# Two-layer hybrid encoder: splits of the left factors placed two products apart, two of them in the down stage, the down stage's first weights fetched and split inside the last pair

## The chip, the cores and the metric

The kernel runs on one core of one Trainium2 chip. The metric is device time of one execution in microseconds (us). Five engines work side by side, each through its own instructions in program order: TensorE (PE, matmuls; its weight loads are listed as PEld), VectorE (DVE), ScalarE (ACT), GpSimd (POOL) and SyncE (SP, which here issues DMA transfers). POOL issues DMA transfers too. A matmul writes to PSUM banks; ACT and DVE copy from there to SBUF.

## The reference, cut to what matters

Two layers, each a token mixer (Fourier mixing, spatial gating, attention) and then a SwiGLU channel mixer, on x of 1024 positions by 1024 channels in float32. The change touches the channel mixer alone:

```python
D_MODEL, SEQ, DEPTH, D_FF = 1024, 1024, 2, 2816

def swiglu(h, w_gate, w_up, w_down):
    return (jax.nn.silu(h @ w_gate) * (h @ w_up)) @ w_down

for l in range(DEPTH):
    ...
    h = rmsnorm(x, g_pre_ffn[l])
    f = swiglu(h, w_gate[l], w_up[l], w_down[l])
    x = x + rmsnorm(f, g_post_ffn[l])
```

## The kernel before, in words

Every float32 factor is split into a rounded high part and the low rest (`split`: a cast on ACT, line 127, then a subtraction on DVE, line 128), and each product is three matmul passes (`matmul3`, line 152): high by high, high by low, low by high. Large products are multiplied by a Strassen scheme with seven products instead of eight.

The channel mixer of a layer has two stages. The **ff stage** computes gate and up in 11 pairs p = 0 to 10 of 256 hidden columns. A pair is 14 products n = 14p + j: j // 2 is the Strassen product v (0 to 6), j % 2 chooses gate or up. `ff_prod(n)` issues 12 matmuls of 128x512 into PSUM tiles fx (the running sum X) or fy (Y and Z); `ff_post(n)` brings them to SBUF: for v = 0, 3 and 4 ACT copies X (line 1050) into a place in the large tile `nat`, and PE goes on adding to the same bank only after that copy. `ff_prep(n + 6)` splits the weights `w_f` of a product six ahead (raw weights `raw_f` lie in a pool `rawp` of 4 buffers).

The result of a pair becomes the left side of the **down stage**. `left_sums` (line 992, on POOL at j = 1 and 3 of the following pair) forms sums of its four blocks, and `left_split(p, k)` splits the seven left factors k = 0 to 6 of pair p; we write 9/k3 for factor 3 of pair 9. The high part goes to one of two places HIS in `nat`, in turn, the low part replaces the source, and `store_a` stores both to a DRAM scratch `asp` (line 986, SP queue, 256 KB each). Since there are two HIS places, a split's cast must wait until the stores of the split two before it have landed. Factors of pair 10 go another way: both parts into one `rawp` buffer, tile `ls`, stored with one transfer of 512 KB, and their splits run in the down stage.

The tables LSTEPS say after which product a split is written in the program. In the last pair they stand at other products than in the ones before. The program is reordered afterwards: a planner with costs of its own moves each engine's instructions, as far as data and order edges allow. `run` leaves the planner free, `run_behind` adds an order edge: what it issues stays, on its engine's queue, behind the instructions written last before it on PE, ACT, DVE and POOL. An order edge is no wait on the chip.

The down stage multiplies by w_down in four groups of 2, 3, 3 and 3 pairs and seven Strassen products each (steps s = 0 to 27). `d_load` fetches 512 KB of w_down into tiles `dr` (line 1080, SP queue); `d_left(s)` fetches stored left factors into tiles `da` (line 1090, POOL queue, 512 KB for each pair); `d_prep(s)` forms the sums of `dr` (line 1100, DVE) and splits them into `dw`; `d_prod` multiplies (PSUM tiles fX, fY), and ACT (line 1144) or DVE (line 1146) brings results to `nat`. Step 0 uses pairs 0 and 1, whose factors were stored long before. The `dr` and `da` tiles take the memory of the ff stage's right factors B11, B21, T1 to B22 (tiles hB, hT), one after the other as these are used up. The table DLOADS says at which of the last products they are fetched: the first four `dr` and the first two `da` are written into the last pair.

Of the kernel before, what the change touches and what calls it, by code (L numbers as in the profile page):

```python
# [81 lines left out]
def encoder_kernel(ctx, tc, A, out):  # L82
# [43 lines left out]
    def split(hi, lo, src, eng=nc.vector):  # L126
        nc.scalar.copy(hi, src)  # L127
        eng.tensor_tensor(out=lo, in0=src, in1=hi.bitcast(F32), op=ALU.subtract)  # L128
# [126 lines left out]
    @contextmanager  # L255
    def behind(*engines):

        with ExitStack() as s:
            ins = nc.cur_bb.bb.instructions
            for eng in engines or (nc.tensor, nc.scalar, nc.vector, nc.gpsimd):  # L260
                prev = next((i for i in reversed(ins) if i.engine == eng.engine), None)
                if prev is not None:
                    s.enter_context(tc.issue_after(prev))
            yield

    def run_behind(*steps):
        with behind():
            run(*steps)
# [15 lines left out]
    def run(*steps):  # L284
        for s in steps:
            s[0](*s[1:])
# [77 lines left out]
    for l in range(DEPTH):  # L364
# [446 lines left out]
        for m in range(1, len(groups)):  # L811
            for j in range(4):
                s = max(8 * m + 2 * j - 9, 0)
# [3 lines left out]
        for n, G in enumerate(groups):  # L817
# [4 lines left out]
            for kt in range(NT):  # L822
                s = 8 * n + kt
# [89 lines left out]
        NPAIR = NFF // 2  # L913
        NPROD = 14 * NPAIR
# [22 lines left out]
        def ff_load(p, m, kh):  # L937
            w = A[("w_gate", "w_up")[m]]
            raws[p, m, kh] = fetch(w[l, kh * 512:(kh + 1) * 512, p * 256:(p + 1) * 256].rearrange("(k p) n -> p k n", p=P), [4, 256],
                                   f"f{l}_{p}_{m}_{kh}")  # L940
# [20 lines left out]
        def ff_prep(n):  # L961
            if n >= NPROD:
                return
            if n + 2 < NPROD and n % 14 < 12:
                ff_sums(n + 2)
            p, j = divmod(n, 14)
            v, m = j // 2, j % 2
            a11, a21, a12, a22 = blocks_of(p, m)
            wv[n] = wsplit((a11, a12, sums.get((p, m)), a11, a21, a22, a12)[v], [4, P], f"f{l}_{n}")
# [6 lines left out]
        def place(i, half):  # L976
            return nat[:, i, half * 512:(half + 1) * 512]
# [4 lines left out]
        def store_a(p, v, x, t, n=1):  # L982

            gi = next(g for g in range(len(DGROUPS)) if p in DGROUPS[g])
            dst = asp[asp_rows(gi, v, p - DGROUPS[gi][0], x, n), :]
            nc.sync.dma_start(dst if n == 1 else dst.rearrange("(x p) n -> p x n", p=P), t)
# [17 lines left out]
        def left_split(p, k):  # L1004

            v, key, m = LEFTS[k]
            t = pq["s", p] if m is None else pq[key, p, m]
            if p == NPAIR - 1:
                w = rawp.tile([P, 2, 512], R32, tag="raw", name=f"ls{l}_{p}_{k}")
                split(w[:, 0], w[:, 1], t)  # L1010
                store_a(p, v, 0, w.bitcast(F32), 2)
                return
            hi = place(*HIS[hin[0] % 2]).bitcast(R32)
            hin[0] += 1
            lo = t.bitcast(R32)
            split(hi, lo, t)
            store_a(p, v, 0, hi.bitcast(F32))
            store_a(p, v, 1, t)

        def ff_prod(n):  # L1020
            p, j = divmod(n, 14)
            v, m = j // 2, j % 2
            if v == 0:
                pq["X", p, m] = psx(f"fx{l}_{n}")
            if v in (1, 2):
                pq["YZ"[v - 1], p, m] = ps1(f"fy{l}_{n}")
            ps = pq["X", p, m] if v in (0, 3, 4, 5) else pq["Y" if v == 1 else "Z", p, m]
            new = v in (0, 1, 2)
            b = hv[RHS[v]]
            for k in range(4):  # L1030
                matmul3(ps, lambda x: wv[n][:, x, k, :], lambda y: b[:, y, k, :], new and k == 0, k == 3, skip_group_check=not new)

        def ff_post(n):
            p, j = divmod(n, 14)
            v, m = j // 2, j % 2
            X = pq["X", p, m]

            def finish(key, acc):

                t = pq[key, p, m]  # L1040
                nc.vector.tensor_tensor(out=t, in0=acc, in1=t, op=ALU.add)  # L1041
                if m == 0:
                    nc.scalar.activation(t, t, AF.Silu)
                else:
                    nc.vector.tensor_tensor(out=t, in0=pq[key, p, 0], in1=t, op=ALU.mult)

            if v in (0, 3, 4):
                key = ("p1", None, None, "u2", "u3")[v]
                t = pq[key, p, m] = pc(p, key, m)
                nc.scalar.copy(t, X)  # L1050
            if v == 1:
                finish("p1", pq["Y", p, m])
            elif v == 4:
                finish("u3", pq["Z", p, m])
            elif v == 5:
                if m == 0:
                    t = pq["s", p] = pc(p, "s")
                    nc.scalar.activation(t, X, AF.Silu)
                else:
                    t = pq["s", p]  # L1060
                    nc.vector.tensor_tensor(out=t, in0=X, in1=t, op=ALU.mult)
            elif v == 6:
                finish("u2", pq["Z", p, m])
# [6 lines left out]
        def d_unit(kind, i, shape, dt, name):  # L1070
            p = du[kind]
            return p.tile([P] + shape, dt, tag=f"{kind}{i}", name=name, bufs=1)
# [19 lines left out]
        def d_blk(gi, pi, b):  # L1092

            r, c = divmod(b, 10)
            return draw[gi, pi, r - 1][:, (c - 1) * 512:c * 512]

        def d_sums(gi, v):
            for pi in range(len(DGROUPS[gi])):
                w = lambda b: d_blk(gi, pi, b)
                tt = lambda o, x, y: nc.vector.tensor_tensor(out=o, in0=x, in1=y, op=ALU.subtract)  # L1100
                if v == 5:
                    tt(w(11), w(12), w(11))
                    tt(w(12), w(22), w(12))
                elif v == 6:
                    tt(w(11), w(22), w(11))
                elif v == 4:
                    tt(w(21), w(21), w(11))
# [6 lines left out]
        def d_prep(s):  # L1114
            if s >= len(STEPS):
                return
            gi, v = STEPS[s]
            d_sums(gi, v)
            for pi in range(len(DGROUPS[gi])):
                nm = f"dw{l}_{s}_{pi}"  # L1120
                if gi + 1 < len(DGROUPS) or v not in DSLOT:
                    t = Wp.tile([P, 2, 512], R32, tag="w", name=nm)
                else:
                    kind, i = DSLOT[v]
                    t = d_unit(kind, i + pi, [2, 512], R32, nm)
                split(t[:, 0], t[:, 1], d_blk(gi, pi, DRIGHT[v]))
                dop[s, pi] = t
# [38 lines left out]
        for t in range(2, NT):  # L1166
# [11 lines left out]
            if t == 7:  # L1178
# [3 lines left out]
                q = res[t]  # L1182
# [19 lines left out]
                  6: ((t_split, "T4", 0), (ff_prep, 12)), 7: ((t_split, "T4", 1), (ff_prep, 13)),  # L1202
                  8: ((t_split, "B22", 0),), 9: ((t_split, "B22", 1),)}

        LSTEPS = {(False, j): ((q, k),) for j, q, k in ((4, 1, 0), (6, 1, 1), (8, 1, 2), (10, 1, 3), (12, 1, 4), (0, 2, 5), (2, 2, 6))}
        LSTEPS.update({(True, j): ((q, k),) for j, q, k in ((4, 1, 0), (5, 1, 1), (7, 1, 2), (8, 1, 3), (9, 1, 4), (11, 1, 5), (12, 1, 6), (0, 2, 5), (2, 2, 6))})
        DLOADS = {0: ((d_load, 0, 0), (d_load, 0, 1)), 1: ((d_left, 0),), 2: ((d_load, 0, 2),), 3: ((d_load, 0, 3),), 5: ((d_left, 1),)}
        for n in range(NPROD):
            p, j = divmod(n, 14)
            ff_prod(n)  # L1210
            if n > 4:
                ff_post(n)
            if n in (0, 2):
                b_tp(6 + n // 2)
            for e in TSTEPS.get(n, ()):
                run_behind(e)
            if j in LOADS and p + 1 < NPAIR:
                ff_load(p + 1, *LOADS[j])
            if p and j in (1, 3):
                left_sums(p - 1, j // 2)  # L1220
            for q, k in LSTEPS.get((p == NPAIR - 1, j), ()):
                if p - q >= 0:
                    left_split(p - q, k)
            if n > 7:
                ff_prep(n + 6)
            if n == NPROD - 10:
                sB.close()
                sL = ExitStack()
                du["wE"] = pool(f"dE{l}", 1, "left", sL)
            if n >= NPROD - 10:  # L1230
                run(*DLOADS.get(n - (NPROD - 10), ()))
        sT.close()


# [2 lines left out]
        du["wO"] = pool(f"dO{l}", 1, "right", sD)  # L1237
        d_left(2)
        d_left(3)
        for s in range(3):  # L1240
            d_prep(s)
        for i in range(2):
            left_sums(NPAIR - 1, i, nc.vector)

# [38 lines left out]
        for s, (gi, v) in enumerate(STEPS):  # L1283
# [8 lines left out]
            k = DORD.index(v)  # L1292
# [54 lines left out]
```

## Time and profile before

| what | value |
|---|---|
| three runs | 2236.36, 2240.76, 2242.62 us; median 2240.76 |
| profiled execution | 2240.43 us, of which the profile's span is 2238.5 us |
| PE busy | 2174.1 us, 97% of the span |
| DVE, ACT, POOL busy | 73%, 51%, 39% |
| granted TensorE clock, mean of the span | 0.99 |
| HBM traffic | 201.22 MB read, 97.52 MB written |

Times in the timeline are from the start of the span. The ff stage of layer 0 runs from about 465 to 907 us, its down stage after that; in layer 1 the ff stage ends near 2018 us. In a timeline row stand the start, the length, engine, line, operation, tiles and the count of merged instructions, and in brackets the idle time of that engine just ahead with what ended it.

### The profile page before, as it was taken

To read this page: it belongs to the slowest core of one execution; us is meant where nothing else is said; L and a number is where in the kernel's file an instruction comes from. 1 tells how busy PE (TensorE), PEld (TensorE's weight loads), DVE (VectorE), ACT (ScalarE), POOL (GpSimd) and SP (SyncE) were. 2 spreads that over 40 slices of the span, in tenths; PEclk is the share of its full clock that TensorE was granted. 3 is DMA by queue.
4 is the path that set the end of the run, shared out by engine and by line. 5 is a ranking of instruction groups with operands and counts; after the bars stand their busy time and mean duration, and the time that the engine had idled before them with its cause. 6 is when DMAs were issued, how large, how long until landed. Compare 5 with 4: busy or idle time off the path is not lost. (4 is left out here: it accounts for less than half of the span.)

```text
span 2238.5 us, 29666 instructions
## 1 busy us (share of the span) xinstructions
PE 2174.1 (97%) x10460; PEld 1799.8 (80%) x10460; DVE 1640.4 (73%) x2579; ACT 1136.9 (51%) x2176; POOL 869.4 (39%) x829
## 2 busy tenths in 40 slices
PE   8999999999999998999999999999999999989997
PEld 7787888877888887888887788888778888868886
DVE  6768986578767675767777698965887676757676
ACT  6338996554444444423352489865544444434232
POOL 2643442235544443222337235322355454522221
PEclk9999999999999999999999999999999999999999
DMA  4110003213535346996631000032145453569865
GB/s 162 39 50 20 11 20 104 100 60 129 183 119 176 134 162 212 331 314 183 215 121 34 17 20 20 11 132 85 57 142 173 129 180 124 179 211 363 275 197 180
DMA packets 171971, 300.66 MB, mean 134 GB/s; under 512 B 17328, under 2 KB 67760, under 8 KB 171824
## 3 DMA queue, kind: packets, MB, share of 16 engines
q1 hardware_dynamic: 128496, 213.31, 27.8%
q0 software_dynamic: 43328, 85.47, 12.4%
q8 instruction: 82, 1.34, 0.3%
q14 instruction: 65, 0.53, 0.1%
HBM read 201.22 MB, written 97.52 MB: 133 GB/s over the span
## 5 line engine op out<-in xcount | busy, mean ns | idle before, releaser
L152 PE MATMUL fx<-hT,w_f 128*128 128x512 f32 x1584 | 379.5, 396 | 22.5 <-ACT nat L1050 20.4
L152 PEld LDWEIGHTS fx<-hT,w_f 128*128 128x128 f32 x1584 | 302.6, 191 | 89.0 <-ACT nat L1050 22.8
L152 PE MATMUL z<-w_z,hT 128*128 128x512 f32 x1152 | 281.5, 398 | 7.8 <-DVE ra_q L437 4.6
L128 DVE TENSOR_TENSOR w_f<-raw_f,w_f 128x512 fp32r<-128x512 f32 x264 | 238.0, 910 | 34.8 <-ACT w_f L127 32.5
L152 PEld LDWEIGHTS z<-w_z,hT 128*128 128x128 f32 x1152 | 213.6, 190 | 54.0 <-DVE ra_q L437 5.4
L152 PE MATMUL fy<-hB,w_f 128*128 128x512 f32 x1056 | 249.6, 391 | 3.2 <-DVE hB L128 3.2
L152 PE MATMUL fX<-dw,da 128*128 128x512 f32 x1056 | 243.8, 389 | 0.0
L127 ACT CAST w_f<-raw_f 128x512 fp32r<-128x512 f32 x264 | 162.2, 621 | 144.9 <-PE fy L152 106.8
L152 PEld LDWEIGHTS fy<-hB,w_f 128*128 128x128 f32 x1056 | 199.1, 189 | 45.6 <-DVE hB L128 4.1
L1090 POOL DMA_DIRECT2D da<-asp x154 | 110.7, 724 | 312.7 <-PE fX L152 155.1
L152 PEld LDWEIGHTS fX<-dw,da 128*128 128x128 f32 x1056 | 198.6, 188 | 41.4
L992 POOL TENSOR_TENSOR nat<-nat 128x512 f32<-128x512 f32 x80 | 127.3, 1613 | 231.0 <-ACT w_f L127 216.9
L128 DVE TENSOR_TENSOR nat<-nat 128x512 fp32r<-128x512 f32 x140 | 158.5, 1155 | 76.5 <-ACT nat L127 73.3
L127 ACT CAST dw<-dr 128x512 fp32r<-128x512 f32 x154 | 94.7, 622 | 232.8 <-PE fX L152 106.3
L127 ACT CAST nat<-nat 128x512 fp32r<-128x512 f32 x140 | 85.2, 621 | 228.3 <-DMA asp<-nat 157.0
L128 DVE TENSOR_TENSOR pT<-ptr,pT 128x512 fp32r<-128x512 f32 x256 | 171.8, 685 | 35.2 <-ACT pT L127 32.8
L152 PE MATMUL fY<-dw,da 128*128 128x512 f32 x792 | 182.9, 389 | 0.0
L760 PE MATMUL pv<-pT,vv 128*128 128x512 f32 x512 | 181.0, 434 | 0.3 <-DVE pT L128 0.3
L152 PEld LDWEIGHTS fY<-dw,da 128*128 128x128 f32 x792 | 148.6, 188 | 30.9
L1041 DVE TENSOR_TENSOR nat<-fy,nat 128x512 f32<-128x512 f32 x132 | 90.7, 688 | 109.4 <-PE fy L152 66.2
L127 ACT CAST pT<-ptr 128x512 fp32r<-128x512 f32 x256 | 150.5, 595 | 39.0 <-PE ptr L748 36.7
L731 DVE TENSOR_REDUCE mx<-sc 128x1 f32<-128x1024 f32 x128 | 155.9, 1219 | 9.4 <-PE sc L728 7.4
(212 smaller groups left out, 3958.8 us busy)
## 6 DMA issues: line engine op xcount, KB each, us to landing
da<-asp POOLq DMA_DIRECT2D x154, 512.0 KB, 6.2
asp<-nat SPq DMA_DIRECT2D x280, 256.0 KB, 3.2
raw_f<-in_w_gate_dram SPq DMA_DIRECT2D x44, 512.0 KB, 3.9
raw_f<-in_w_up_dram SPq DMA_DIRECT2D x44, 512.0 KB, 4.6
dr<-in_w_down_dram SPq DMA_DIRECT2D x44, 512.0 KB, 6.8
xin<-xs SPq DMA_DIRECT2D x24, 512.0 KB, 5.2
raw_z<-in_w_in_dram SPq DMA_DIRECT2D x16, 512.0 KB, 4.7
raw_wo<-in_w_out_dram SPq DMA_DIRECT2D x16, 512.0 KB, 3.9
```

The lines of the kernel that those rows point to most:

```text
L127: nc.scalar.copy(hi, src)
L128: eng.tensor_tensor(out=lo, in0=src, in1=hi.bitcast(F32), op=ALU.subtract)
L152: nc.tensor.matmul(ps, lhs(a), rhs(b), start=first and i == 0, stop=last and i == 2, **kw)
L731: nc.vector.tensor_reduce(mx, sc, axis=AX.X, op=ALU.min)
L760: nc.tensor.matmul(pv, vv[:, kt, g].rearrange("p i d -> p (i d)"), pT[:, i], start=(kt == 0 and i == 0), stop=(kt == 7 and i == 1))
L992: tt = lambda o, x, y, op: eng.tensor_tensor(out=o, in0=x, in1=y, op=op)
L1041: nc.vector.tensor_tensor(out=t, in0=acc, in1=t, op=ALU.add)
L1090: nc.gpsimd.dma_start(t[:, pi], asp[asp_rows(gi, v, pi, 0, 2), :].rearrange("(x p) n -> p x n", p=P))
```

## The change

Four things change, in both layers. The splits of pairs 1 to 9 are written with `run_behind`, two products apart, and the last pair uses the same table as the others. The factors k = 5 and 6 of pair 9 go through `rawp` like those of pair 10 and are written in the down stage. The first weights of the down stage may be fetched from three products earlier on: the four `d_load` stand after j = 2 to 5 of the last pair, the two `d_left` after j = 7 and 9 (before: `d_load` at j = 4, 4, 6, 7, `d_left` at j = 5 and 9). And `d_prep(0)`, the first split of w_down, is written after product j = 11 of the last pair, with `run_behind`.

```diff
-            if p == NPAIR - 1:
+            if p == NPAIR - 1 or k > 4 and p == NPAIR - 2:
                 w = rawp.tile([P, 2, 512], R32, tag="raw", name=f"ls{l}_{p}_{k}")
                 split(w[:, 0], w[:, 1], t)
                 store_a(p, v, 0, w.bitcast(F32), 2)
...
-        LSTEPS = {(False, j): ((q, k),) for j, q, k in ((4, 1, 0), (6, 1, 1), (8, 1, 2), (10, 1, 3), (12, 1, 4), (0, 2, 5), (2, 2, 6))}
-        LSTEPS.update({(True, j): ((q, k),) for j, q, k in ((4, 1, 0), (5, 1, 1), (7, 1, 2), (8, 1, 3), (9, 1, 4), (11, 1, 5), (12, 1, 6), (0, 2, 5), (2, 2, 6))})
-        DLOADS = {0: ((d_load, 0, 0), (d_load, 0, 1)), 1: ((d_left, 0),), 2: ((d_load, 0, 2),), 3: ((d_load, 0, 3),), 5: ((d_left, 1),)}
+        LSTEPS = {j: ((q, k),) for j, q, k in ((4, 1, 0), (6, 1, 1), (8, 1, 2), (10, 1, 3), (12, 1, 4), (0, 2, 5), (2, 2, 6))}
+        DLOADS = {1: ((d_load, 0, 0),), 2: ((d_load, 0, 1),), 3: ((d_load, 0, 2),), 4: ((d_load, 0, 3),), 6: ((d_left, 0),), 8: ((d_left, 1),)}
...
-            for q, k in LSTEPS.get((p == NPAIR - 1, j), ()):
+            for q, k in LSTEPS.get(j, ()):
                 if p - q >= 0:
-                    left_split(p - q, k)
+                    run_behind((left_split, p - q, k))
...
-            if n == NPROD - 10:
+            if n == NPROD - 13:
                 sB.close()
                 sL = ExitStack()
                 du["wE"] = pool(f"dE{l}", 1, "left", sL)
-            if n >= NPROD - 10:
-                run(*DLOADS.get(n - (NPROD - 10), ()))
+            if n >= NPROD - 13:
+                run(*DLOADS.get(n - (NPROD - 13), ()))
+            if n == NPROD - 3:
+                run_behind((d_prep, 0))
...
-        for s in range(3):
+        for s in range(1, 3):
             d_prep(s)
+        for i in (5, 6):
+            left_split(NPAIR - 2, i)
```

What this makes of the order on the engines is seen at three places of layer 0 (layer 1 has the same rows). The first is ACT's queue around the last weight splits w_f 152 and 153. A cast nat<-nat is the first half of a split of a left factor, a copy nat<-fx frees the running sum for PE, and dw is the first weight of the down stage. Before:

```order
L1043 ACTIVATE nat_68<-nat_68 128x512
L127 CAST nat_68<-nat_68 128x512
L127 CAST w_f0_152_8106<-raw_f0_10_0_1_7790 128x512
L127 CAST nat_68<-nat_68 128x512 x2
L127 CAST w_f0_153_8128<-raw_f0_10_1_1_7809 128x512
L127 CAST nat_68<-nat_68 128x512 x3
L1050 COPY nat_68<-fx0_140_7956 128x512
L127 CAST dw0_0_0_8246<-dr0_0_0_8065 128x512
L1050 COPY nat_68<-fx0_141_7977 128x512
L127 CAST dw0_0_1_8249<-dr0_0_1_8067 128x512
L1050 COPY nat_68<-fx0_140_7956 128x512
```

and now:

```order
L127 CAST nat_68<-nat_68 128x512 x2
L127 CAST w_f0_152_8107<-raw_f0_10_0_1_7790 128x512
L127 CAST w_f0_153_8123<-raw_f0_10_1_1_7809 128x512
L1050 COPY nat_68<-fx0_140_7956 128x512
L127 CAST nat_68<-nat_68 128x512
L1050 COPY nat_68<-fx0_141_7977 128x512
L1050 COPY nat_68<-fx0_140_7956 128x512
L1043 ACTIVATE nat_68<-nat_68 128x512
L127 CAST nat_68<-nat_68 128x512
L1050 COPY nat_68<-fx0_141_7977 128x512
L1058 ACTIVATE nat_68<-fx0_140_7956 128x512
L127 CAST nat_68<-nat_68 128x512
```

Six casts of left factors stood ahead of the first copy of fx 140 after w_f 151, three of them directly; now two stand ahead of it, and the others, 9/k1 to 9/k3 by their count, are spread between the copies. Directly behind the last row shown now come the four casts of dw.

The second place is SP's queue after the last raw weights: stores to asp and loads dr. Before:

```order
L137 DMA raw_f0_10_1_1_7809<-in_w_up_dram 128x4x256
L986 DMA asp_81<-nat_68 128x512 x15
L1080 DMA dr0_0_0_8065<-in_w_down_dram 128x1024
L1080 DMA dr0_0_1_8067<-in_w_down_dram 128x1024
L1080 DMA dr0_0_2_8109<-in_w_down_dram 128x1024
L1080 DMA dr0_0_3_8131<-in_w_down_dram 128x1024
L986 DMA asp_81<-nat_68 128x512 x4
```

and now:

```order
L986 DMA asp_81<-ls0_9_6_8264 128x2x512
L986 DMA asp_81<-nat_68 128x512 x4
L1080 DMA dr0_0_0_8024<-in_w_down_dram 128x1024
L1080 DMA dr0_0_1_8046<-in_w_down_dram 128x1024
L1080 DMA dr0_0_2_8069<-in_w_down_dram 128x1024
L1080 DMA dr0_0_3_8088<-in_w_down_dram 128x1024
L1080 DMA dr0_2_4_8775<-in_w_down_dram 128x1024
L1080 DMA dr0_2_5_8777<-in_w_down_dram 128x1024
L986 DMA asp_81<-nat_68 128x512 x6
L1080 DMA dr0_1_0_8304<-in_w_down_dram 128x1024
```

Six loads of 512 KB, which stood behind the stores of 9/k0 to 9/k4 or behind all of pair 9, now stand ahead of the stores of 9/k1 to 9/k3 (the x6), and the stores of 9/k5 and 9/k6 (ls) stand ahead of them all.

The third place is DVE's queue from the last addition of fy 145 (ff stage) to the first addition of a down product, fY 1_0 (line 1146), whose bank PE needs again in step 2. Before:

```order
L1041 TENSOR_TENSOR nat_68<-fy0_145_8069,nat_68 128x512
L128 TENSOR_TENSOR dw0_4_0_8363<-dr0_0_2_8109,dw0_4_0_8363 128x512
L1045 TENSOR_TENSOR nat_68<-nat_68 128x512
L992 TENSOR_TENSOR nat_68<-nat_68 128x512 x3
L128 TENSOR_TENSOR dw0_4_1_8366<-dr0_0_3_8131,dw0_4_1_8366 128x512
L992 TENSOR_TENSOR nat_68<-nat_68 128x512
L128 TENSOR_TENSOR dw0_5_0_8416<-dr0_0_0_8065,dw0_5_0_8416 128x512
L1146 TENSOR_TENSOR nat_68<-fY0_1_0_8327,nat_68 128x512
```

and now, from the second row after that addition:

```order
L128 TENSOR_TENSOR nat_68<-nat_68 128x512
L1100 TENSOR_TENSOR dr0_0_1_8046<-dr0_0_3_8088,dr0_0_1_8046 128x512
L128 TENSOR_TENSOR dw0_2_0_8254<-dr0_0_0_8024,dw0_2_0_8254 128x512
L1045 TENSOR_TENSOR nat_68<-nat_68 128x512
L128 TENSOR_TENSOR dw0_2_1_8257<-dr0_0_1_8046,dw0_2_1_8257 128x512
L1100 TENSOR_TENSOR dr0_0_0_8024<-dr0_0_2_8069,dr0_0_0_8024 128x512
L992 TENSOR_TENSOR nat_68<-nat_68 128x512 x2
L1100 TENSOR_TENSOR dr0_0_1_8046<-dr0_0_3_8088,dr0_0_1_8046 128x512
L1100 TENSOR_TENSOR dr0_0_2_8069<-dr0_0_2_8069,dr0_0_0_8024 128x512
L992 TENSOR_TENSOR nat_68<-nat_68 128x512
L128 TENSOR_TENSOR dw0_3_0_8310<-dr0_0_0_8024,dw0_3_0_8310 128x512
L1146 TENSOR_TENSOR nat_68<-fY0_1_0_8327,nat_68 128x512
```

Eight instructions stood between the two additions, now thirteen do (one of them, a sum of dr, comes ahead of the rows shown). The work itself is the same; in the order before, part of it stood ahead of the addition of fy 145. On PE, the six matmuls of fX that stood between fx products 148 and 149 now stand behind the last ff product. On POOL, the order of `left_sums` and of the loads da is unchanged here.

## The prediction

> **What bounds the kernel now.** I read the page's first block, then the waits of PE, then the timeline around the longest of them.
>
> ```profile
> span 2238.5 us, 29666 instructions
> PE 2174.1 (97%) x10460; PEld 1799.8 (80%) x10460; DVE 1640.4 (73%) x2579; ACT 1136.9 (51%) x2176; POOL 869.4 (39%) x829
> PE fx L152 <- ACT nat L1050: 20.4, 6, 8.6
> PE sc L728 <- ACT pj L741: 7.6, 6, 1.8
> ```
>
> PE is the bound: it is busy for all but 64 us. In the list of waits (us in total, times, longest) one group stands out, fx waiting for the copy that frees the running sum. The same list over the ff stage of each layer (500 to 920, 1600 to 2060 us) has one long wait in each:
>
> ```profile
> PE fx L152 <- ACT nat L1050: 7.4, 1, 7.4
> PE fx L152 <- ACT nat L1050: 8.6, 1, 8.6
> ```
>
> PE's timeline there, layer 0 and then layer 1, and three stretches of 5 us in layer 0 (busy time of PE, PEld, DVE, ACT, POOL, then granted clock, DMA share, GB/s):
>
> ```profile
> 868.07 5.60 PE L152 MATMUL fy<-hT,w_f 128*128 128x512 f32 x24
> 873.51 5.60 PE L152 MATMUL fx<-hT,w_f 128*128 128x512 f32 x24
> 886.50 5.49 PE L152 MATMUL fx<-hT,w_f 128*128 128x512 f32 x12 [7.38 <-ACT nat L1050]
> 891.78 1.86 PE L152 MATMUL fX<-dw,da 128*128 128x512 f32 x6
> 901.22 2.88 PE L152 MATMUL fx<-hT,w_f 128*128 128x512 f32 x12
> ...
> 1998.40 4.56 PE L152 MATMUL fx<-hT,w_f 128*128 128x512 f32 x12 [8.56 <-ACT nat L1050]
> 2002.80 1.55 PE L152 MATMUL fX<-dw,da 128*128 128x512 f32 x6
> 875.00:880.00 5.00, 4.11 (x19) 3.06 (x17) 0.82 (x2) 1.24 (x2) 0.99 (x2) 1.00 1.08 353
> 880.00:885.00 5.00, 0.00 (x0) 0.00 (x0) 0.54 (x1) 0.00 (x0) 0.85 (x2) 0.72 1.19 402
> 885.00:890.00 5.00, 3.50 (x8) 2.81 (x9) 2.11 (x4) 2.82 (x5) 0.00 (x0) 0.50 1.10 400
> ```
>
> PE stands from 879.1 to 886.5, in the midst of the last pair, after fx 147 (the second of the 24 at 873.51); the clock falls to 0.50, and the next product takes 5.49 us where the same twelve matmuls take 2.88 at 901.22. Why the copy came late is in ACT's timeline, with SP's and POOL's beside it:
>
> ```profile
> 871.09 1.14 ACT L127 CAST nat<-nat 128x512 fp32r<-128x512 f32 x2 [2.14 <-DVE nat L128]
> 878.52 1.29 ACT L127 CAST nat<-nat 128x512 fp32r<-128x512 f32 x2 [5.77 <-DMA asp<-nat]
> 885.34 0.62 ACT L127 CAST nat<-nat 128x512 fp32r<-128x512 f32 x1 [5.53 <-DMA asp<-nat]
> 885.86 0.58 ACT L1050 COPY nat<-fx 128x512 f32<-128x512 f32 x1
> 867.75 12.41 SPq L986 DMA_DIRECT2D asp<-nat  x9
> 880.27 2.07 SPq L1080 DMA_DIRECT2D dr<-in_w_down_dram  x4
> 870.41 1.53 POOL L1090 DMA_DIRECT2D da<-asp  x2
> 873.98 1.43 POOL L1090 DMA_DIRECT2D da<-asp  x2 [2.04 <-PE fy L152]
> 879.42 1.43 POOL L1090 DMA_DIRECT2D da<-asp  x2 [4.01 <-PE fx L152]
> ```
>
> Fx 140 had been ready for its copy since about 876.3 (half of the 24 matmuls), but the copy stood on ACT's queue behind three casts of left factors. Each needs a HIS place whose stores have landed, and these crawled: loads da of 1 MB each started at 870.4, 874.0 and 879.4, and the DMA moved 353 to 402 GB/s. So the stall is one of order, not of work.
>
> **The change part by part.** *The copies pass the casts (ACT).* The first ACT piece of the front part shows two casts, 8/k6 and 9/k0, left ahead of the copy of fx 140. Both have their data early: 9/k0 is a sum of POOL's four L992, which end where da starts, at 870.4. The places they need were used by 8/k4 and 8/k5, two to four products earlier. The copy then starts at 876.3, and fx 148 follows fx 147 without a gap. What goes is the wait and the slow stretch behind it: in layer 0 7.38 + (5.49 - 2.88) + (1.86 - 1.55) = 10.30 us, in layer 1 8.56 + (4.56 - 2.88) = 10.24 us; in sum 20.5 us. A stall inside pairs 1 to 9 can't go, since there is none:
>
> ```profile
> 600.00:700.00 100.00, 100.00 (x443) 82.81 (x442) 72.41 (x82) 46.98 (x84) 51.43 (x35) 1.00 0.47 163
> 809.42 0.62 ACT L127 CAST nat<-nat 128x512 fp32r<-128x512 f32 x1 [2.09 <-DMA asp<-nat]
> ```
>
> [...]
>
> *The spacing.* The same casts and subtractions run, 5.44 us apart (24 matmuls, 868.07 to 873.51), so a HIS place is used again after 10.9 us. Their stores land, by the page, in
>
> ```profile
> asp<-nat SPq DMA_DIRECT2D x280, 256.0 KB, 3.2
> ```
>
> 3.2 us (median), and the casts now wait about 2 us each (809.42). I cost it at nothing; the cover is 10.9 - 3.2 = 7.7 us, and if it is gone the copies of fx stand behind a cast again.
>
> *Two factors through rawp.* 9/k5 and 9/k6: two casts, two subtractions as before, two stores of 512 KB for four of 256 KB. The buffer is that of raw weights whose last user, the split w_f 148, stands ahead on both queues. Nothing.
>
> *The w_down loads ahead of the stores (SP).* This is what may cost. SP reaches the first dr behind the stores of 9/k0, whose low part is ready about 870.5 (POOL's end plus a subtraction), instead of at 880.27. From 870.4 on there are then in flight: da for steps 0 and 1, four transfers; six dr; and in SP's order behind them the store of 9/k1's high part, issued near 877.5 (cast behind the copy at 876.3). With 0.524 MB each and three stores of 0.262 MB (9/k0 twice, 9/k1) that is 10 x 0.524 + 3 x 0.262 = 6.03 MB. At the 400 GB/s of the row above it takes 15.1 us: the store lands at **885.5** if all is served in order of issue. If POOL's loads of steps 2 and 3 (issued at 879.4, and near 885 when fx 149 is done) get in ahead, it is 5.2 us more: **890.7**. I take the middle, 888; the rows nearest to it are the loads dr of the same stretch, min, median and max from issue to landing:
>
> ```profile
> DMA to landing us min/median/max: 3.4/6.5/10.1
> ```
>
> 877.5 + 10.1 = 887.6. What needs it: 9/k3 takes the place of 9/k1, and ACT has the four casts of dw behind 9/k3. PE reaches the first fX when its six ff products 148 to 153 are done, 72 x 5.44 / 24 = 16.3 us after 879.1, at 895.4. Casts come every 0.55 us (871.09: two in 1.14), DVE's halves every 0.60; so with 9/k3 at X the last of the four dw is split on ACT at X + 2.8 and on DVE about 0.7 later, and PE needs the first at 895.4 and the low parts within a microsecond of that. X may be 892. Cost 0 up to 890.7, which my upper bound just meets.
>
> [...]
>
> *DVE behind the end of the ff stage.* The third piece shows thirteen instructions between the addition of fy 145 and that of fY 1_0 where eight stood. In before:
>
> ```profile
> 907.31 0.69 DVE L1041 TENSOR_TENSOR nat<-fy,nat 128x512 f32<-128x512 f32 x1 [0.68 <-PE fy L152]
> 908.58 0.69 DVE L1045 TENSOR_TENSOR nat<-nat 128x512 f32<-128x512 f32 x1
> 913.23 0.68 DVE L1146 TENSOR_TENSOR nat<-fY,nat 128x512 f32<-128x512 f32 x1
> ```
>
> There 9 starts took 913.23 - 907.31 = 5.9 us, 0.66 each with a small wait. PE in the changed order: 48 matmuls of steps 0 and 1 follow 895.4, 10.9 us, so it wants the bank of fY 1_0 at 906.3. DVE may start the addition of fy 145 at 895.4, or by its queue at 896.4 (line 1061 needs fx 151, 58 matmuls or 13.1 us after 879.1, at 892.2; then seven starts of 0.60); 14 starts of 0.60 later, 904.8, comes fY 1_0, done at 905.5. The margin is 0.8 us. At 0.66 each it is gone: 906.3. I cost it at 0.5 us a layer, bounds 0 and 3 (a wait of DVE for the cast of 9/k4, which stands among these rows).
>
> *The first dw.* Written behind j = 11, it stands behind 9/k3 and no longer ahead of the copies of fx; needed at 895.4, see above. Nothing beyond that.
>
> *The sum.* -20.5 + 2 x 0.5 = -19.5 against the profiled execution, 2240.43, gives 2220.9. The median of the three runs is 0.3 us above that execution; I predict **2221**. The terms' own bounds are 2220 (nothing given back) to 2226 (3 a layer).
>
> **The rivals.**
> [...]
> *B, DVE's backlog.* The margin of 0.8 us fails and PE waits at fY 2_0 to 2_3 by 2 to 4 us in each layer: 2224 to 2228. For: 0.66 us in the row above. Against: PE's step 3 can only be late once by the same backlog.
> *C, the stall only moves.* X at 902 or later would give back all of 10.3 us, 2238 to 2241. It takes a store of 24 us; the casts' longest wait for one was 6.8 us in before (total, times, longest):
>
> ```profile
> ACT nat L127 <- DMA asp<-nat: 157.0, 63, 6.8
> ```
>
> *D, slower.* The order edge holds a cast just ahead of the copy of fx 127 and its like in every pair (9/k1 ahead of fx 141 in the ACT piece). If its place is not free, PE waits in 10 pairs of 2 layers. The price that decides is 20.5 / 20 = 1.0 us a pair; at 1.5 us it is 2250. Against: the 7.7 us of cover; for: only that the copy of the second product of v = 3 has 2.7 us to spare.
>
> **How the numbers follow.** Forecast (20 us less a little, 2219 to 2224) 0.74; A 0.10; B 0.08; C 0.03; D 0.05. A run tells 0.3%, 6.7 us, from no change. The forecast, B and A but for 0.01 of its far end make faster, 0.91; that 0.01, C and 0.01 of D at its weak end make the same, 0.05; the rest of D is slower, 0.04. The range goes from 2215 (the forecast and the 4 us by which the fastest run lay below the median) to 2233, which leaves out C, D and the far end of A.
>
> **What would show it.** In the profile after: the long wait of fx for L1050 is gone in both layers and the granted clock at 880 to 890 stays near 1; casts nat<-nat stand singly on ACT, waiting less than 2 us for asp; dr starts near 871 to 874; PE passes from fy to fX near 895 with no idle time above 1 us. [...] The prediction is wrong if PE's waits in either layer's ff stage and steps 0 to 3 sum to more than 4 us.

## The result, and the profile after

The changed kernel takes 2221.03 us (median of four runs, 2219.90 to 2222.47) where the kernel before takes 2240.65 (2236.36 to 2242.62) on the same chip: ratio 0.9913, 95% interval 0.9902 to 0.9925. Predicted were 2221 us. The profiled execution took 2221.81 us, 2219.7 of them the span. First the head of its page, PE's row and, from the list of PE's waits (us in total, times, longest), the row that was 20.4, 6, 8.6:

```profile
span 2219.7 us, 29668 instructions
PE 2168.9 (98%) x10460; PEld 1796.1 (81%) x10460; DVE 1640.0 (74%) x2579; ACT 1134.9 (51%) x2176; POOL 872.9 (39%) x829
PE fx L152 <- ACT nat L1050: 4.5, 4, 1.2
```

Two of the six waits are gone, the long ones; the four that stay (4.4 us before, 4.5 now) lie at the start of the two ff stages and are not touched by the change. PE's timeline through the last pair of layer 0 and into steps 0 and 1, and then the end of the same stretch in layer 1:

```profile
875.36 13.76 PE L152 MATMUL fx<-hT,w_f 128*128 128x512 f32 x60
897.12 0.84 PE L152 MATMUL fX<-dw,da 128*128 128x512 f32 x3
909.23 4.33 PE L152 MATMUL fY<-dw,da 128*128 128x512 f32 x18 [1.07 <-ACT dw L127]
...
1974.21 13.76 PE L152 MATMUL fx<-hT,w_f 128*128 128x512 f32 x60
2007.58 4.36 PE L152 MATMUL fY<-dw,da 128*128 128x512 f32 x18 [0.56 <-ACT dw L127]
```

Sixty matmuls run in one piece where PE stood still after the first 24, and the granted clock (the eighth figure from the left, counts in brackets left out, ahead of DMA share and GB/s) holds through the stretch where it was 0.72 and 0.50:

```profile
880.00:885.00 5.00, 5.00 (x24) 4.14 (x23) 0.84 (x2) 1.18 (x2) 1.43 (x2) 1.00 1.11 400
885.00:890.00 5.00, 5.00 (x24) 4.14 (x23) 2.12 (x4) 2.33 (x4) 1.43 (x2) 1.00 1.10 379
```

What replaced the stall is small and stands two steps later. The rows of ACT, SP and DVE behind it:

```profile
878.28 0.59 ACT L1050 COPY nat<-fx 128x512 f32<-128x512 f32 x1 [4.82 <-PE fx L152]
893.00 0.62 ACT L127 CAST nat<-nat 128x512 fp32r<-128x512 f32 x1 [3.23 <-DMA asp<-nat]
893.52 2.18 ACT L127 CAST dw<-dr 128x512 fp32r<-128x512 f32 x4
899.99 1.14 ACT L127 CAST dw<-dr 128x512 fp32r<-128x512 f32 x2
873.90 3.46 SPq L1080 DMA_DIRECT2D dr<-in_w_down_dram  x6
879.41 15.29 SPq L986 DMA_DIRECT2D asp<-nat  x6
895.21 0.69 DVE L128 TENSOR_TENSOR dw<-dr,dw 128x512 fp32r<-128x512 f32 x1 [0.87 <-ACT dw L127]
900.03 0.68 DVE L1041 TENSOR_TENSOR nat<-fy,nat 128x512 f32<-128x512 f32 x1
908.45 1.28 DVE L1146 TENSOR_TENSOR nat<-fY,nat 128x512 f32<-128x512 f32 x2
```

The copy of fx 140 now waits for PE, not PE for it. The cast of 9/k3 (893.00) still waits 3.23 us for the store of 9/k1 behind the six dr; the four casts of dw follow it, DVE's subtraction waits for the first of them, and fourteen starts after the addition of fy 145 (900.03) DVE begins that of fY 1_0 (908.45), which frees PE's bank at 909.1, a tenth before PE resumes. The row of PE names ACT's dw as the releaser of the 1.07 us; the two casts for this product had ended at 901.1 (899.99 + 1.14), and the addition L1146 is the one that fits.

### The profile page after: what moved, and what is told of

It is laid out like the page before. It is cut to its first block, busy times and chain, and to the rows that moved or that the text cites. A ratio compares the mean times of both kernels' runs of the same rounds, so it can differ in the third digit from the quotient of the medians.

```text
span 2219.7 us, 29668 instructions
## 1 busy us (share of the span) xinstructions
PE 2168.9 (98%) x10460; PEld 1796.1 (81%) x10460; DVE 1640.0 (74%) x2579; ACT 1134.9 (51%) x2176; POOL 872.9 (39%) x829
## 5 line engine op out<-in xcount | busy, mean ns | idle before, releaser
L152 PE MATMUL fx<-hT,w_f 128*128 128x512 f32 x1584 | 373.7, 392 | 6.8 <-ACT nat L1050 4.5
L128 DVE TENSOR_TENSOR w_f<-raw_f,w_f 128x512 fp32r<-128x512 f32 x264 | 247.1, 944 | 26.6 <-ACT w_f L127 24.8
L128 DVE TENSOR_TENSOR nat<-nat 128x512 fp32r<-128x512 f32 x136 | 147.5, 1094 | 122.2 <-ACT nat L127 121.8
L1050 ACT COPY nat<-fx 128x512 f32<-128x512 f32 x132 | 77.7, 589 | 170.6 <-PE fx L152 163.5
L748 PE MATMUL ptr<-identr,pj 128*128 128x128 f32 x1024 | 154.3, 273 | 0.9 <-ACT pj L741 0.8
```

Source lines behind the costliest of these rows:

```text
L152: nc.tensor.matmul(ps, lhs(a), rhs(b), start=first and i == 0, stop=last and i == 2, **kw)
L748: nc.tensor.transpose(tr[:, j * P:(j + 1) * P], ast["p", G, j][:, kt * P:(kt + 1) * P], ident)
```

## The experiments

Theory: the stall is one of order. A copy of fx stands on ACT's queue behind casts of left factors, these wait for HIS places, and the places' stores crawl because loads share the DMA with them. What wins is that the order edges keep those casts behind the copies in the last pair. Rivals: the earlier loads or the first split of w_down do it; the spacing of the splits in all pairs does it; the edges cost in pairs 1 to 9; the stores are slow by themselves.

### One part without the other

**The spacing, the two moved factors and the edges alone.** The changed kernel with the old times for the loads and `d_prep(0)`:

```diff
-        DLOADS = {1: ((d_load, 0, 0),), 2: ((d_load, 0, 1),), ... 8: ((d_left, 1),)}
+        DLOADS = {0: ((d_load, 0, 0), (d_load, 0, 1)), 1: ((d_left, 0),), ... 5: ((d_left, 1),)}
...
-            if n == NPROD - 3:
-                run_behind((d_prep, 0))
...
-        for s in range(1, 3):
+        for s in range(3):
             d_prep(s)
```

> The changed kernel, but w_down is fetched from j = 4 on as before, and the first split of w_down is written after the loop without an order edge. Its planned order holds the cast of the first dw ahead of the copy of fx 140 on ACT; SP's queue stands as in the changed kernel. Theory (the gain is that the copies of fx no longer stand behind six casts): most of the gain stays; dr of step 0 is issued near 874 and lands near 880 to 882, so the copy waits 0 to 2 us a layer for it: 2219 to 2226 us. Rival (the early loads and the first dw inside the last pair bring the gain): 2232 to 2241.

Measured: 2220.86 us, 0.9909 (0.9894 to 0.9924). The whole gain is there without the other two edits. It was nearer to the edge than the time tells: here the planner put the first cast of dw, which waits for its load, ahead of the copy of fx 140.

```profile
879.04 0.62 ACT L127 CAST dw<-dr 128x512 fp32r<-128x512 f32 x1 [6.02 <-DMA dr<-in_w_down_dram]
879.57 0.58 ACT L1050 COPY nat<-fx 128x512 f32<-128x512 f32 x1
874.91 8.36 PE L152 MATMUL fx<-hT,w_f 128*128 128x512 f32 x36
```

The copy ended at 880.15, and the 36 matmuls, whose third dozen needs it from about 880.3 (874.91 + 5.44 us for 24 matmuls), have no gap. With the casts of dw this early, ahead of 9/k3, PE has no wait at fX or fY behind them either, in both layers; the waits of 1.07 and 0.56 us are there only with the other two edits.

**The loads and the first split alone.** The kernel before with those two edits (the same lines, in reverse):

> The kernel before with the new table of early loads and the first split of w_down written after j = 11 with an order edge; the splits of left factors stay as before. Its planned order on ACT still holds six casts ahead of the copy of fx 140, and dr stands behind the stores of 9/k0 to 9/k4 on SP. Theory: the stall of 7 to 9 us stays in both layers, 2237 to 2244 us. Rival (the early loads bring the gain): below 2232.

Measured: 2240.61 us, ratio 1.0000 (0.9992 to 1.0009). The stall stands; PE's waits in the last pair and the first steps of layer 0, and the PE row behind it:

```profile
PE fx L152 <- ACT nat L1050: 7.9, 1, 7.9
891.99 5.49 PE L152 MATMUL fx<-hT,w_f 128*128 128x512 f32 x12 [7.94 <-ACT nat L1050]
```

So the early loads and the first split of w_down are worth nothing that can be measured, and the splits' edges, spacing and moved factors together all of it.

### The edges, and where they count

**No edges on the splits.** The changed kernel with

```diff
-                    run_behind((left_split, p - q, k))
+                    left_split(p - q, k)
```

> The changed kernel with the same table and the same two factors moved, but the splits written without order edges, so that the planner moves them forward again: four casts ahead of the copy of fx 140 instead of six (before) or two (changed). Theory: two of the casts wait for stores in the loaded stretch, 2 to 5 us of stall a layer at the copies of fx, also because dr now stands behind all stores of pair 9 on SP and dw ahead of the copy of fx 141: 2224 to 2234 us. Rival (the table alone is enough, the edges do nothing): 2219 to 2223. Rival (two factors moved away do nothing): 2237 to 2242.

Measured: 2241.14 us, 1.0003 (0.9993 to 1.0014): a miss on the bad side, since I had left the new table some of the gain; it lies where the last rival has it, so the table and the two moved factors win nothing without the edges. Here the planner pulls the casts forward again, and the dr stand behind eight stores on SP. PE, ACT and SP in layer 0:

```profile
888.63 1.22 PE L152 MATMUL fX<-dw,da 128*128 128x512 f32 x2 [4.57 <-ACT dw L127]
889.66 7.45 PE L152 MATMUL fx<-hT,w_f 128*128 128x512 f32 x24
879.89 0.62 ACT L127 CAST nat<-nat 128x512 fp32r<-128x512 f32 x1 [6.17 <-DMA asp<-nat]
887.97 0.62 ACT L127 CAST dw<-dr 128x512 fp32r<-128x512 f32 x1 [6.97 <-DMA dr<-in_w_down_dram]
868.72 12.14 SPq L986 DMA_DIRECT2D asp<-nat  x8
```

A cast waits 6.17 us and holds the copy by 1.4 us only, but then the first cast of dw waits 6.97 us, because its load was issued near 881. Most of the stall is there under another name: 1.42 us for the copy, 4.57 us for dw, then 24 matmuls in 7.45 us instead of 5.60. (The profiled execution, 2237.00 us, was the quickest of twelve that go up to 2246.99. Its profile shows the kind of stall; where the slower ones lose the rest is not shown.)

**Edges in the last pair alone, and everywhere but there.**

```diff
-                    run_behind((left_split, p - q, k))
+                    (run_behind if p == NPAIR - 1 else run)((left_split, p - q, k))
```

> The changed kernel, but the splits of the left factors are written with order edges in the last pair alone; pairs 1 to 9 are left to the planner as before the change. Theory (what counts is which casts stand ahead of the four copies of fx in the last pair): the whole gain stays, 2218 to 2224 us, ratio 0.990 to 0.993, and the profile has no wait for L1050 above 2 us in either layer. Rival (the spacing in pairs 1 to 9 matters too, because it clears the stores ahead of the last pair): part of the stall is back, 2226 to 2241.

Measured: 2220.81 us, 0.9908 (0.9893 to 0.9922). The complement swaps `run` and `run_behind`:

> The complement: order edges in pairs 1 to 9, none in the last pair, where the planner puts a third and a fourth cast ahead of the copy of fx 140 and the casts of dw between the copies, with the first dr behind eight stores of left factors on SP. Theory: the gain is gone, 2236 to 2243, ratio 0.998 to 1.001, with a wait of 4 us or more in each layer, for L1050 or for the cast of dw. Rival (spaced stores in pairs 1 to 9 are what frees the places): most of the gain stays, 2220 to 2230.

Measured: 2236.33 us, 0.9985 (0.9975 to 0.9994). PE in layer 0 and layer 1, and ACT in layer 0:

```profile
883.20 4.62 PE L152 MATMUL fx<-hT,w_f 128*128 128x512 f32 x12 [3.26 <-ACT nat L1050]
890.34 4.61 PE L152 MATMUL fx<-hT,w_f 128*128 128x512 f32 x12 [2.52 <-ACT nat L1050]
...
1991.47 5.49 PE L152 MATMUL fx<-hT,w_f 128*128 128x512 f32 x12 [4.71 <-ACT nat L1050]
882.04 0.62 ACT L127 CAST nat<-nat 128x512 fp32r<-128x512 f32 x1 [7.19 <-DMA asp<-nat]
```

The last pair decides. All that the change does without the edges there, those of pairs 1 to 9 included, is the 0.15% of this row (0.06 to 0.25%). That these edges cost nothing clear of the scatter (rival D) is the row before: 2220.81 us without them, 2221.03 with. The one profile without them has no wait at fY: its last cast ahead of dw comes 16.6 us after the row of sixty matmuls starts (890.50 and 873.94), not 17.6. Whether the edges or chance made this microsecond is not shown.

**The old dense table, with edges.** All of pair 9 goes through the HIS places inside the last pair, and sixteen stores stand ahead of the dr on SP's queue:

```diff
-            if p == NPAIR - 1 or k > 4 and p == NPAIR - 2:
+            if p == NPAIR - 1:
...
+        LSTEPS.update({(True, j): ((q, k),) for j, q, k in ((4, 1, 0), (5, 1, 1), (7, 1, 2), (8, 1, 3), (9, 1, 4), (11, 1, 5), (12, 1, 6), (0, 2, 5), (2, 2, 6))})
...
-        for i in (5, 6):
-            left_split(NPAIR - 2, i)
```

> The changed kernel with order edges everywhere, but with the old dense table for the last pair: all seven factors of pair 9 go through the two HIS places inside the last pair, so that three casts stand ahead of the copy of fx 140 (two in the changed kernel), two ahead of dw behind the last copy (one), and sixteen stores ahead of the six dr. Theory: the third cast comes when the fourth did before the change, near 879, so fx waits at most 1 us; but the two casts ahead of dw wait for stores that crawl behind the dr, so dw is 2 to 6 us late and PE waits for it at fX in both layers: 2223 to 2233, taken 2227. Rival 1 (the edges alone do it; dense or spaced is the same): 2218 to 2223. Rival 2 (without spacing nothing is won): 2236 to 2243.

Measured: 2222.63 us, 0.9917 (0.9903 to 0.9932). By its time rival 1 holds (2218 to 2223): this is just below the range of the theory and 4 us below the value I took. The mechanism of the theory is there on a small scale, layer 0 on ACT and PE and layer 1 on PE:

```profile
897.61 0.62 ACT L127 CAST nat<-nat 128x512 fp32r<-128x512 f32 x1 [2.21 <-DMA asp<-nat]
898.80 1.21 PE L152 MATMUL fX<-dw,da 128*128 128x512 f32 x4 [1.07 <-ACT dw L127]
...
1999.12 1.20 PE L152 MATMUL fX<-dw,da 128*128 128x512 f32 x4 [2.02 <-ACT dw L127]
```

The last cast ahead of dw comes at 897.61 instead of 893.00, and PE waits for dw at fX, 1.07 and 2.02 us. The price of a late dw was sized too high, since PE wants only the first of the four casts when it gets to fX (it starts at 898.80, and the first of four casts ends at 898.75), not all of them 2.8 us after the last cast of a left factor. The spacing and the two moved factors are worth 1.6 us by the medians, within what the runs scatter.

### The rest of the loss

**The first split of w_down two products earlier** (`n == NPROD - 5` for `NPROD - 3`), so that the casts of dw stand ahead of the late 9/k3:

> The changed kernel with the first split of w_down written after j = 9 instead of 11, so that its four casts stand ahead of 9/k3 on ACT, which waited 3.2 us for the store of 9/k1. Theory (the late store held the dw casts, these DVE, and DVE the bank of fY 2_0): the waits of fY of 1.1 and 0.6 us go, 2218.5 to 2221. Rival (DVE's own count of instructions sets it): the waits stay, 2220 to 2222.5. Rival (the four dr have not landed by then and hold the copies): over 2223.

```profile
885.16 2.18 ACT L127 CAST dw<-dr 128x512 fp32r<-128x512 f32 x4
890.39 0.62 ACT L127 CAST nat<-nat 128x512 fp32r<-128x512 f32 x1 [2.40 <-DMA asp<-nat]
895.36 5.60 PE L152 MATMUL fX<-dw,da 128*128 128x512 f32 x24
900.80 9.68 PE L152 MATMUL fY<-dw,da 128*128 128x512 f32 x42
```

Measured: 2220.47 us, 0.9913 (0.9899 to 0.9926). The waits at fY are gone in both layers, as they must be if the late cast is their root. The time, whose runs go from 2218.05 to 2224.92, can't show 1.6 us.

### Why the stores crawl

**The loads of da later.** The kernel before with `d_left(0)` and `d_left(1)` written behind the last pair (which also puts their tiles in another pool and the first split of w_down behind an order edge):

> The kernel before the change, but the first two loads of stored left factors (da, 2 x 1 MB) are taken from the last pair to behind it, so that they start some 8 us later; the planner still puts four casts of left factors ahead of the copy of fx 140. Theory (the stores crawl because these loads fill the DMA): the stores before 879 land in 4 us or less, the casts pass, fx waits for L1050 at most 2 us in each layer, and a wait of 0 to 4 us for da at fX may come instead: 2220 to 2232. Rival (two places and the chain cast, subtraction, store make the casts slow whatever else the DMA does): the wait for L1050 stays at 6 to 9 us and the time at 2236 to 2248.

Measured: 2243.39 us, 1.0005 (0.9996 to 1.0015). This doesn't decide the question. The planner started the first da at 874.50 (870.41 before), and it put six dr between the stores in their stead, so the DMA had no less to do (a mean of 267 GB/s from 866 to 882 us, 243 before):

```profile
873.69 1.91 SPq L986 DMA_DIRECT2D asp<-nat  x3
875.69 1.86 SPq L1080 DMA_DIRECT2D dr<-in_w_down_dram  x2
874.50 1.53 POOL L1090 DMA_DIRECT2D da<-asp  x2 [3.51 <-PE fy L152]
878.74 0.62 ACT L127 CAST nat<-nat 128x512 fp32r<-128x512 f32 x1 [5.47 <-DMA asp<-nat]
916.42 4.58 PE L152 MATMUL fY<-dw,da 128*128 128x512 f32 x12 [4.15 <-ACT dw L127]
```

The cast waits 5.47 us as ever. The stall came out at other places: 0.26 and 1.94 us for the copies, 1.95 for dw at fX and 4.15 at fY, in layer 0.

**No loads of da.** The kernel before, with one line changed: POOL writes zeros instead, so the left factors of steps 0 and 1 are left out of the output. Order and code of ACT up to the copy, and of SP, stay as they are:

```diff
-                    nc.gpsimd.dma_start(t[:, pi], asp[...])
+                    nc.gpsimd.memset(t[:, pi].bitcast(F32), 0.0) if s < 2 else nc.gpsimd.dma_start(t[:, pi], asp[...])
```

> The kernel before the change, order of ACT up to the copy of fx 140 and all of SP as it was, but the left factors of steps 0 and 1 of the down stage are not fetched: POOL writes zeros into those da tiles instead, so 2 MB of loads in each layer fall away around 870 to 880 us, and those two products are left out of the output. Six casts still stand ahead of the copy. Theory (the stores crawl because these loads share the DMA with them): ACT's waits for a store between 870 and 890 fall from 5.5 and 5.8 us to 3 us or less, the wait of fx for L1050 in the last pair from 7.4 and 8.6 to 2 us or less, and the time is 2218 to 2227 us although nothing was moved. Rival (two places and the chain of cast, subtraction and store are slow by themselves): the wait stays at 6 to 9 us, 2236 to 2242.

Measured: 2222.88 us, 0.9919 (0.9904 to 0.9934). ACT in layer 0, PE's row, and the stores of the window 866 to 882 us (count, size, median us to landing), of this kernel:

```profile
876.31 1.24 ACT L127 CAST nat<-nat 128x512 fp32r<-128x512 f32 x2 [1.07 <-DMA asp<-nat]
880.33 0.62 ACT L127 CAST nat<-nat 128x512 fp32r<-128x512 f32 x1 [2.77 <-DMA asp<-nat]
875.99 8.54 PE L152 MATMUL fx<-hT,w_f 128*128 128x512 f32 x36
asp<-nat SPq DMA_DIRECT2D x13, 256.0 KB, 2.1
```

and of the kernel before, in the same window:

```profile
asp<-nat SPq DMA_DIRECT2D x9, 256.0 KB, 5.4
```

All six casts still stand ahead of the copy. Their waits fall from 5.77 and 5.53 us to 1.07 and 2.77, and the copy is in time. So the stall needs both: the casts ahead of the copy, and the loads beside the stores. Taking away either gives the same 18 to 20 us.

**One more megabyte.** The changed kernel, with a copy of 1 MB issued by POOL behind the first da (shortened):

```diff
+                n == NPROD - 7 and run_behind(*[(nc.gpsimd.dma_start, more[...], asp[...]) for pi in range(2)])
```

> The changed kernel, and POOL issues, directly behind the loads of da for step 0, a copy of 1 MB from the scratch of left factors to another place in DRAM that nothing reads. Nothing else in the last pair is moved. Theory (the store of 9/k1 lands late by what stands ahead of it in the DMA): at 400 GB/s 1 MB takes 2.6 us, or twice that if reading and writing both count; the last cast ahead of dw, 9/k3, comes at 895.5 to 898 instead of 893.0 and PE waits 3 to 7 us in all at fX or fY in each layer instead of 1.6 and 0.8: 2224 to 2233. Rival (the store's landing does not depend on it): the cast stays within 0.7 us of 893 and the time at 2218 to 2223.

Measured: 2227.60 us, 0.9935 (0.9918 to 0.9952), 6.6 us above the changed kernel. ACT and PE in layer 0, then PE in layer 1:

```profile
895.19 0.62 ACT L127 CAST nat<-nat 128x512 fp32r<-128x512 f32 x1 [5.30 <-DMA asp<-nat]
911.43 5.96 PE L152 MATMUL fY<-dw,da 128*128 128x512 f32 x18 [2.18 <-ACT dw L127]
...
2013.32 4.37 PE L152 MATMUL fY<-dw,da 128*128 128x512 f32 x18 [2.18 <-ACT dw L127]
```

This span runs 0.13 us behind that of the changed kernel there (fx at 875.49 and 875.36), so 9/k3 comes 2.06 us later for 1 MB, a little under the 2.5 to 5 expected. PE's wait at fY doubles or more in both layers; the waits are 2.9 us in layer 0 (0.67 of it at fX) and 3.6 in layer 1 (1.4 of it for da, later in the down stage), just under and inside the 3 to 7 us expected (the changed kernel has 1.07 and 0.8; the 1.6 of the expectation is both layers' fY). In layer 0 the slow clock (0.75 from 910 to 915 us) goes with 1.6 us more for eighteen matmuls (5.96 for 4.33).

## Why the prediction was right, point by point

- *The copies pass the casts, -20.5 us*: right in mechanism and size. On the clock of before (the last pair starts 1.85 us later in the changed profile, 875.36 for 873.51, what is left of 2.36 us from the mixer) the copy starts at 876.4; predicted 876.3. The spans differ by 18.8 us; -20.5 and the waits below make -18.7.
- *The spacing and the two moved factors, 0*: right as a cost. As causes they are nearly empty too (2222.63 without both, 2241.14 with both and no edges).
- *The store of 9/k1, X = 888*: mis-sized. Measured 893.00 - 1.85 = 891.15, just outside the bounds of 885.5 to 890.7 and inside the limit of 892. The error was the landing time: the store went out when it was said to (879.41 - 1.85 = 877.6; predicted 877.5), and I gave it 10.1 us, the longest landing of a dr before; it took 13.6 (893.00 - 879.41). Part of it is that the transfers ahead began later than the sum has them: the first dr at 872.1, not behind a low part ready about 870.5. Dw was not late for PE by it, but it was for DVE.
- *DVE behind the end, 0.5 us a layer*: mis-sized by the same error. I let DVE start the addition of fy 145 at 896.4; it started at 900.03 - 1.85 = 898.2, 1.8 late, because the subtraction of dw ahead of it waited for ACT. Less the margin of 0.8 that is 1.0; measured 1.07 in layer 0 and 0.56 in layer 1 (and 0.2 for da, later in the down stage), 1.8 in all against 1.0. The late store of 9/k1 (A) and DVE's backlog (B), to which I gave separate chances, are one chain.
- *The chances*: D, held copies in every pair, did not come; the edges in pairs 1 to 9 cost nothing clear of the scatter. C, the stall that only moves, did not come either, but the run without edges on the splits shows that it was real: it gave back everything.
- *What would show it*: dr at 873.90 - 1.85 = 872.1, fX at 895.3 without a gap, the clock at 1.00, all as said. Not as said: the last cast waited 3.23 us (2.72 in layer 1), above 2. And by its last sentence the prediction would be wrong, but that bound of 4 us on PE's waits in a layer was badly drawn: they sum to 6.6 and 5.9, but 5.5 of the 6.6 in layer 0 lie early in the ff stage, where the kernel before has them too (5.3) and I had not counted them.
- *The two ends of X*: 885.5 has all transfers in order of issue, 890.7 has POOL's loads of steps 2 and 3 ahead; the measured 891.15 lies just above the upper end. What the two queues moved there, by the packets that the profile counts on SP's queue (q1) and POOL's (q0), first in the changed kernel from 880 to 886 us, then in the run with one more megabyte from 881 to 884 (packets, MB, share of 16 engines):

```profile
q1 hardware_dynamic: 430, 1.56, 69.7%
q0 software_dynamic: 430, 0.83, 41.6%
...
q0 software_dynamic: 93, 0.96, 76.2%
q1 hardware_dynamic: 91, 0.31, 26.6%
```

  In the changed kernel the two queues have the same number of packets in this stretch, 430 each, but not the same bytes: SP's packets, most of them of the loads dr, were 3.6 KB on average and POOL's 1.9, so SP's queue moved 65% of the bytes. The kernel before shows the same from 885 to 889 us (285 and 282 packets, 1.04 and 0.54 MB). In the run with one more megabyte the counts are again nearly equal (93 and 91), but POOL's packets were 10 KB on average, and SP's queue moved 0.31 MB where the changed kernel moves 0.77 from 881 to 884 (216 packets, POOL's queue 217). At that rate the missing 0.46 MB are 1.8 us, an estimate that covers most of the 2.06. By which rule the DMA takes the packets is not shown.
- *Luck*: the ff stage of layer 0 starts 2.36 us later in the changed profile (467.88 for 465.52), and the early ff stage of layer 1 gives 3.0 us the other way (the profiles lie 7.03 us apart at its first matmul, 10.03 at its last pair). Neither is a term of the forecast; that they nearly cancel is luck. So is it that the medians meet the forecast to 0.1 us, with the terms 0.8 us off (-18.7 for -19.5).

## What to carry to other kernels

When the bounding engine waits for a cheap copy, read what stands ahead of that copy on its queue and what that waits for, down to the transfer: here three casts stood ahead and 2 MB of loads made their stores slow, and taking away either gave the same 1%. An order edge on work that may be late, placed where a planner would pull it forward, was worth all that the runs can tell from their scatter of a four-part change; without it the other parts won nothing. After such an edit look for the next queue where the late thing stands ahead of something needed (here dw behind 9/k3), since a stall that is only renamed gives nothing, as the run without edges showed.

## What was not expected of the hardware

The same short wait went with a slow clock in one layer and with the full one in the other. With the wait of 2.18 us at fY in the run with one more megabyte goes a granted clock of 0.75 in layer 0 and of 1.00 in layer 1 (length, busy time of PE, PEld, DVE, ACT, POOL, clock, DMA share, GB/s):

```profile
910.00:915.00 5.00, 3.57 (x11) 2.85 (x12) 5.00 (x10) 4.26 (x9) 0.99 (x2) 0.75 1.23 403
2010.00:2015.00 5.00, 2.82 (x13) 2.02 (x12) 5.00 (x10) 4.30 (x9) 1.43 (x2) 1.00 1.12 399
```

It is so with shorter ones. In layer 1 of the run without edges on the splits a wait of 1.94 us is followed by twelve matmuls in 4.61 us (clock 0.92 from 1985 to 1990 us, 0.74 from 1990 to 1995); in layer 0 of the run with later loads of da, one of 1.94 us by twelve in 3.01 (clock 1.00 from 890 to 900 us), where 2.88 is their time in the kernel before at a clock of 1.00 (901.22).

So in these runs the length of a wait alone does not tell whether a slow clock goes with it. Behind the 1.07 us of the changed kernel there was none (1.00 from 905 to 915 us, eighteen matmuls in 4.33 us). What decides it was not measured.
